# First weight block in four loads, later loads held back, idle products in a gap, a row norm moved to VectorE, four operands re-spaced

## The chip, the cores and the metric

The kernel runs on one core of a Trainium2 chip. The metric is device time in microseconds (us), of which the median of three runs is quoted; one more execution was profiled, and all rows come from that one. Engines: PE (TensorE) does the products, PEld its weight loads, DVE is VectorE, ACT is ScalarE, POOL is GpSimd, SP issues most transfers.

## The reference, cut to what matters

Two transformer blocks run one after the other on 256 rows of width 1024, all in float32. The front of the first block, where most of the change lies, is this:

```python
h = rms_norm(x, norm_mix_g)
proj = h @ w_in
q_d, k_d, v_d, conv_in, q_m, gate_logits = jnp.split(proj, SPLIT_POINTS, axis=-1)
...
mem_n = rms_norm(mem, norm_mem_g)
kv = mem_n @ w_mem_kv
k_m, v_m = jnp.split(kv, 2, axis=-1)
k = rms_norm(k_m.reshape(B, M, MEM_HEADS, MEM_HEAD_DIM), mk_norm_g)
...
y_attn = o.reshape(B, S, DIFF_WIDTH) @ w_attn_o
y_conv = short_gated_conv(conv_in, conv_w) @ w_conv_o
merged = g[:, :, 0] * y_attn + g[:, :, 1] * y_conv + g[:, :, 2] * y_mem
x = x + merged @ w_o
```

After it come an MLP, and a second model with grouped attention, an MLP, a gated block and a last MLP.

## The kernel before

Every float32 matrix is split into a high part and a rest, both in the format fp32r, and a product is three: high by high, high by rest, rest by high. Weights come from memory in units of 1 MB (`raw`, three buffers, loaded by SP). ACT copies each half of a unit to its high part `whi`, DVE subtracts to get the rest `wlo` (lines 86 and 87), seven halves ahead of use at most. The activations are split the same way into pairs of tiles: `memh` (the normed memory), `hT` (the normed input), `cvT`, `oT`, `omT` (convolution, first attention, memory attention), `mgT` (the merged branches), `act` (the MLPs). The two shapes of product are these:

- *Column products* (lines 406 to 408; 488, 489 and 491 in the first one): the activation stands in PE, and 512 columns of weights stream by it.
- *Feature products* (lines 506 to 508): the weights stand, and 256 columns of activation stream by. One group of 24 products shares one half unit.

The order of the work is the program's own order on each engine; `tick()` marks a step after each half unit, and `later(n, f)` puts `f` behind `n` such steps. So PE's work in the first 70 us is: eight idle products of a tile of ones, the transposes of the first 128 rows of the memory (`mt0`), 12 products with the first unit, the transposes of the second 128 rows (`mt1`), the rest of the product with `w_mem_kv` (192 products with `memh` in all), and between them the transposes of small vectors (`vr`), of the keys (`kq`) and of the two halves of the normed input (`kn`). The row norm of the input (`in_norm`, then `norm`) sums squares on ACT and takes the reciprocal root by three Newton steps: on POOL if an engine is handed over, else on DVE in nine instructions. The key norm (`evac_m`, `rsqrt`) takes its root on POOL and is applied by DVE (line 723).

`operands(pool, name, n, skip)` allocates such a pair of tiles with 256 spare bytes, and starts the data `skip` bytes into them. In the built program the split weights all start 64 bytes past a multiple of 128. The distance of each activation from that, modulo 128 bytes, is: `act` and `omT` 0, `hT` 64, `memh` 32, `mgT` 16, `oT` 80, `cvT` 48.

Of the kernel before, what the change touches and what calls it, by code (L numbers as in the profile page):

```python
# [8 lines left out]
F32 = mybir.dt.float32  # L9
# [6 lines left out]
P = 128  # L16
# [7 lines left out]
class Weights:  # L24
# [29 lines left out]
    def load(self, n):  # L54
        while self.loaded < min(n, len(self.plan)):
            t = self.raw_pool.tile([P, 2048], F32, tag="raw", name="raw")
            _, _, src, (a, b) = self.plan[self.loaded]
            v = t.rearrange("p (a b) -> p a b", a=a)
            if self.loaded < 1:
                for h in range(2):  # L60
                    k = slice(h * a // 2, (h + 1) * a // 2)
                    self.nc.sync.dma_start(out=v[:, k], in_=src[:, k])
            else:
                self.nc.sync.dma_start(out=v, in_=src)
            self.raw[self.loaded] = v
            self.loaded += 1
# [4 lines left out]

    def pump(self, n=None):
        while self.split < 2 * len(self.plan) and self.split < min(self.used + self.ahead, n or self.cap):
            self.load(self.split // 2 + self.RAW)
            u, h = divmod(self.split, 2)
            kind, key, _, (a, b) = self.plan[u]
            v = self.raw[u]
            if kind == "B":
                v, shape = v[:, :, h * 128:(h + 1) * 128], (8, 128)
            else:  # L80
                v, shape = v[:, h * a // 2:(h + 1) * a // 2, :], (a // 2, b)
            hi = self.split_pool.tile([P, 1024], F32R, tag="hi", name="whi")
            lo = self.split_pool.tile([P, 1024], F32R, tag="lo", name="wlo")
            hv = hi.rearrange("p (a b) -> p a b", a=shape[0])
            lv = lo.rearrange("p (a b) -> p a b", a=shape[0])
            self.nc.scalar.copy(hv, v)  # L86
            self.rests.append(lambda v=v, hv=hv, lv=lv: self.nc.vector.tensor_sub(lv, v, hv.bitcast(F32)))  # L87
            self.ready.append((kind, key, hv, lv))
            self.split += 1
            if h:  # L90
                del self.raw[u]
# [21 lines left out]
def kernel(  # L113
# [8 lines left out]
    nc = tc.nc  # L122
    V, S, T, G = nc.vector, nc.scalar, nc.tensor, nc.gpsimd
    PSUM = bass.MemoryType.PSUM

    def pool(stack, name, bufs=1, side=None, **kw):
        if side:
            kw["side"] = side
        return stack.enter_context(tc.tile_pool(name=name, bufs=bufs, reuse_waits="tile", **kw))

    const = pool(ctx, "const")

    def operands(p, name, n, skip=0, **kw):

        ts = [p.tile([P, 2048 + 64], F32R, name=f"{name}{i}", **({"tag": f"{name}{i}"} if kw else {}), **kw) for i in range(n)]
        return [t[:, skip // 4:skip // 4 + 2048].rearrange("p (k t) -> p k t", t=256) for t in ts]
# [8 lines left out]
    def bank(p=ps_x):  # L145
        return p.tile([P, 512], F32, tag="bank", name="bank")


    W = Weights(nc, w_raw, w_split)
# [54 lines left out]
    ones = const.tile([P, P], F32, name="ones")  # L204
    V.memset(ones, 1.0)
    xt = [const.tile([P, D], F32, name=f"x{t}") for t in range(NT)]
    hT = [const.tile([P, 8, 256], F32R, name=f"hT{i}") for i in range(2)]
    const.tile([P, 8], F32, name="fill")
    right = ExitStack()
    left = ExitStack()  # L210
    pool(ctx, "edge", side="right").tile([P, 8], F32, name="edge")
# [3 lines left out]
    qmT = memp.tile([P, 8, 256], F32, name="qmT")  # L215
    memin_st = ExitStack()
    memin = pool(memin_st, "memin", side="right")
    memh = operands(memin, "memh", 2, 96)
    mt = [memin.tile([P, D], F32, name=f"mt{t}") for t in range(NT)]
    for n in range(2):  # L220
        nc.sync.dma_start(out=mt[0][:, n * 512:n * 512 + 512], in_=mem[0, 0:P, n * 512:n * 512 + 512])
    W.load(1)
    nc.sync.dma_start(out=mt[1], in_=mem[0, P:2 * P, :])
    W.load(3)

    def rows_of(a):
        return a.rearrange("o (k p) -> (o k) p", p=P)
# [35 lines left out]
    mkg = bc("mkg", mk_norm_g, 256)  # L263
    lam4 = memp.tile([P, 4, 64], F32, name="lam4")
    ssm = memin.tile([P, NT, 2], F32, name="ssm")
    for _ in range(8):
        ps = bank()
        T.matmul(ps[:, 0:P], ones, ones, start=True, stop=True)

    def rsqrt(ss, inv, y, E=None):  # L270

# [23 lines left out]
    def tmp(tag, bufs, n=512):  # L295
        return tmp_pool[0].tile([P, n], F32, tag=tag, name=tag, bufs=bufs)
# [41 lines left out]
    def norm(t, src, ssp, gcol, bcol, dst, E=None):  # L338


        h = small.tile([P, 2], F32, tag="nh", name="nh")
        y = small.tile([P, 1], F32, tag="ny", name="ny")
        if E is not None:
            E.tensor_add(h[:, 0:1], ssp[:, 0:1], ssp[:, 1:2])
            rsqrt(h[:, 0:1], 1.0 / D, y, E)
        else:
            u = small.tile([P, 1], F32, tag="nu", name="nu")
            V.tensor_scalar(h[:, 0:1], ssp[:, 0:1], -0.5 / D, -0.5 * EPS, op0=ALU.mult, op1=ALU.add)
            h = V_stt(h[:, 1:2], ssp[:, 1:2], -0.5 / D, h[:, 0:1], ALU.mult, ALU.add)
            V.tensor_scalar(y.bitcast(I32), h.bitcast(I32), -0.5, RSQRT_SEED - (1 << 22) - (1 << 30), op0=ALU.mult, op1=ALU.add)  # L350
            for _ in range(3):
                V_stt(u, y, h, y, ALU.mult, ALU.mult)
                V_stt(y, u, 1.5, y, ALU.add, ALU.mult)

        def part_2():
            xn = [tmp("kn", 2) for _ in range(2)]
            V.tensor_scalar(xn[0], src[:, 0:512], y, None, op0=ALU.mult)
            S.activation(xn[1], src[:, 512:1024], AF.Identity, scale=y)

            return transposed(t, xn, gcol, bcol, dst)  # L360

        return part_2

    def V_stt(o, a, sc, b, op0, op1):
        V.scalar_tensor_tensor(o, a, sc, b, op0=op0, op1=op1)
        return o
# [6 lines left out]
    def later(n, f):  # L373

        due.append((clock[0] + n, f))
# [23 lines left out]
    def drain():  # L399
        run_due(True)  # L400
        while fillers:
            fillers.popleft()()
        run_due(True)
# [185 lines left out]
    def c1(name, i=0, n=1):  # L589
        v, o = col[name]  # L590
        return vt[v][:, o + i:o + i + n]

    def in_norm(t, src, name, dst):
        ssp = small.tile([P, 2], F32, tag="ssp", name="ssp")
        for n in range(2):
            sumsq(src[:, n * 512:n * 512 + 512], ssp[:, n:n + 1])

        def part_1():
            part_2 = norm(t, src, ssp, c1(name, 0, 8), None, dst, G)
            later(2, lambda: later(3, part_2()))  # L600
        return part_1

    memg = c1("mem", 0, 8)
    mem0, mem1 = (transposed(t, [mt[t][:, n * 512:n * 512 + 512] for n in range(2)], memg, None, memh) for t in range(NT))
# [30 lines left out]
    vecs(0)  # L635

    def mem_mid():
        W.pump(2)
        W.rests.popleft()()
        W.rest()  # L640

    mem0(mem_mid)
    lamneg = const.tile([P, 1], F32, name="lamneg")

    sm = small.tile([P, 2], F32, tag="lsm", name="lsm", bufs=1)
# [23 lines left out]
        later(1, lambda: V.tensor_mul(cond, cond, sig))  # L669

    qkg = const.tile([P, 1], F32, name="qkg")
    later(8, small_setup)
    later(7, lam_sums)
    for i in range(8):
        later(i + 1, lambda: load_smalls(5))
    for t in range(NT):
# [269 lines left out]
    for n in range(2):  # L946
        gemm_cols("in", K0 + 512 * n, hT, evac_k(n))
        gemm_cols("in", Q0 + 512 * n, hT, evac_q(n))
        gemm_cols("in", V0 + 512 * n, hT, evac_v(n))
        if n == 0:  # L950
            drain()
            lam_exp()
            kq_st.close()
            right.close()
            attn_st.close()
            attnp = pool(attn_st, "attnd")
            right = ExitStack()
            oTp = pool(right, "oTp", side="right")
            oT = operands(oTp, "oT", 2, 208)
            kq_p[0] = pool(kq_st, "kq2", side="right")  # L960
            slots(8, [[(0, dif_a)], [(4, dif_ot), (1, dif_b)], [(2, dif_o), (3, dif_n)], [(1, dif_t)]])
    run_due(True)
# [1 line left out]


    convp = pool(right, "conv", side="right")
    cvT = operands(convp, "cvT", 2, 176)
    inner_st = ExitStack()
    inner = pool(inner_st, "inner", side="right").tile([P, 2, 258], F32, name="inner")
    dif_banks[0] = ps_a  # L970
# [1 line left out]
    for f in range(4):  # L972
        xc = tmp("kn", 2).rearrange("p (j c) -> p j c", j=2)
        ps = gemm_feat("in", XC + 256 * f, hT)
        S.copy(xc, ps)
        tick()
        ps = gemm_feat("in", GC + 256 * f, hT)
# [9 lines left out]
        ps = gemm_feat("in", GB + 256 * f, hT)  # L987
# [83 lines left out]
    for f in range(5):  # L1071
        if f < 4:
            branch(G1, 1, "co", cvT, f)
            branch(G2, 2, "mo", omT, f)
        if f == 0:
            cond_silu()
        if f == 1:
            drain()
            attn_st.close()
            qkv_st.close()  # L1080
            ada_p[0] = pool(adap_st, "adap")
            mgp = pool(right, "mgT", side="right")
            mgT = operands(mgp, "mgT", 2, 16)
            for j in range(3):
                ada_load(j)
            ada.extend([lambda: None] * 3)
            for j in range(len(ada_order)):
                ada.append(lambda j=j: ada_step(j))
            clock[1] = 1.04
        if f >= 1:  # L1090
            branch(G0, 0, "ao", oT, f - 1, mgT)
# [345 lines left out]
    for i in range(15):  # L1437
        if i < 12:
            ps = gemm_feat("gin", 256 * i, hT, p=ps_x)
# [72 lines left out]
```

## Time and profile before

| what | value |
|---|---|
| median of three runs | 1320.16 us (1317.58 to 1320.21) |
| the profiled execution | 1320.45 us |
| its span, first to last instruction | 1318.7 us |
| PE busy | 1280.7 us, 97% of the span |
| DVE, ACT, POOL busy | 71%, 55%, 11% |
| mean granted TensorE clock | 0.988 |
| memory traffic | 275.43 MB, mean 209 GB/s |

The span leaves out 1.75 us around it. A share of busy time is a mean over stages. PE's busy time counts a product that is in flight, so two kinds of product at different speeds look equally busy; their speed is read from how many start in a stretch.

### The profile page before, as it was taken

How to read it: one execution, taken by the hardware profiler on the slowest of the kernel's cores; microseconds unless marked ns; L12 is line 12 of the kernel's file. 1: busy time of each engine (PE TensorE's matmuls, PEld its weight loads, DVE VectorE, ACT ScalarE, POOL GpSimd, SP SyncE). 2: the span in 40 equal slices, each digit the busy share in tenths (PEclk: the TensorE clock that was granted, in tenths of full speed). 3: DMA queues.
4: the chain of work that ended last, by engine and by line, in shares of the span. 5: the costliest groups of instructions: out<-in, count | busy, mean ns of one | idle time of the engine just before them, and what ended most of it. 6: DMA issues, size and time to landing. Idle time of an engine off the chain costs nothing.

```text
span 1318.7 us, 20492 instructions
## 1 busy us (share of the span) xinstructions
PE 1280.7 (97%) x7883; PEld 1121.9 (85%) x7883; DVE 929.8 (71%) x1416; ACT 725.7 (55%) x1176; POOL 141.6 (11%) x375
## 2 busy tenths in 40 slices
PE   8899999999999999999878999999999999999998
PEld 6688789999998889977655899987889898799897
DVE  5555678856777788677786787786888877764453
ACT  6765675554444655445555666455556544584451
POOL 1522144500001000100310000000000000000000
PEclk8999999999999999999979999999999999999999
DMA  6573345466885798883431588885886775365650
GB/s 235 201 236 115 129 133 163 158 219 204 276 279 185 225 291 301 275 305 128 158 104 42 190 280 280 294 289 190 282 284 208 264 248 192 119 233 192 223 192 32
DMA packets 166958, 275.43 MB, mean 209 GB/s; under 512 B 8412, under 2 KB 95244, under 8 KB 166732
## 3 DMA queue, kind: packets, MB, share of 16 engines
q1 hardware_dynamic: 137260, 219.78, 49.9%
q10 hardware_dynamic: 27808, 50.41, 11.7%
q0 software_dynamic: 1792, 3.92, 1.1%
q8 instruction: 62, 1.02, 0.3%
q14 instruction: 36, 0.29, 0.1%
HBM read 273.04 MB, written 1.05 MB: 208 GB/s over the span
## 4 chain that ended last, share of the span: by engine, by line
PE 71%; DVE 10%; DMA 8%; ACT 5%; POOL 2%; issue 2%; SPq 0%; ACTq 0%; DVEq 0%; POOLq 0%
PE bank L406 12%; PE bank L407 12%; PE bank L408 12%; PE bank L506 9%; PE bank L507 9%; PE bank L508 9%; DMA araw<-in_ada_w_dram 6%; DVE wlo L87 4%; PE bank L456 2%; ACT whi L86 1%; PE bank L1426 1%; DVE gate L1027 1%; ACT p L1279 1%; PE bank L304 1%; PE bank L447 1%
## 5 line engine op out<-in xcount | busy, mean ns | idle before, releaser
L86 ACT CAST whi<-raw 128x1024 fp32r<-128x1024 f32 x412 | 425.7, 1052 | 267.5 <-PE bank L408 57.9
L87 DVE TENSOR_TENSOR wlo<-raw,whi 128x1024 fp32r<-128x1024 f32 x412 | 496.0, 1220 | 83.5 <-ACT whi L86 82.4
L506 PE MATMUL bank<-hT,whi 128*128 128x256 f32 x1152 | 324.7, 282 | 0.0
L507 PE MATMUL bank<-hT,whi 128*128 128x256 f32 x1152 | 321.2, 279 | 0.0
L508 PE MATMUL bank<-hT,wlo 128*128 128x256 f32 x1152 | 321.2, 279 | 0.0
L506 PEld LDWEIGHTS bank<-hT,whi 128*128 128x128 f32 x1152 | 217.0, 188 | 1.9 <-issue 1.3
L508 PEld LDWEIGHTS bank<-hT,wlo 128*128 128x128 f32 x1152 | 218.2, 189 | 0.0
L507 PEld LDWEIGHTS bank<-hT,whi 128*128 128x128 f32 x1152 | 216.4, 188 | 0.6
L407 PE MATMUL bank<-wlo,act 128*128 128x512 f32 x384 | 150.6, 392 | 2.8 <-DVE wlo L87 2.7
L406 PE MATMUL bank<-whi,act 128*128 128x512 f32 x384 | 150.5, 392 | 0.0
L408 PE MATMUL bank<-whi,act 128*128 128x512 f32 x384 | 150.1, 391 | 0.0
L406 PE MATMUL bank<-whi,hT 128*128 128x512 f32 x308 | 126.9, 412 | 0.8 <-ACT hT L330 0.8
L408 PE MATMUL bank<-whi,hT 128*128 128x512 f32 x308 | 121.6, 395 | 0.0
L407 PE MATMUL bank<-wlo,hT 128*128 128x512 f32 x308 | 121.2, 393 | 0.0
L1027 DVE SCALAR_TENSOR_TENSOR acc<-araw,cond,acc 128x512 f32<-128x512 f32 x128 | 95.7, 748 | 34.6 <-DMA araw<-in_ada_w_dram 34.3
L407 PEld LDWEIGHTS bank<-wlo,act 128*128 128x128 f32 x384 | 72.5, 189 | 19.1 <-DVE wlo L87 4.5
L408 PEld LDWEIGHTS bank<-whi,act 128*128 128x128 f32 x384 | 72.5, 189 | 15.1
L406 PEld LDWEIGHTS bank<-whi,act 128*128 128x128 f32 x384 | 72.4, 188 | 14.6
L406 PEld LDWEIGHTS bank<-whi,hT 128*128 128x128 f32 x308 | 58.2, 189 | 17.5 <-ACT hT L330 4.2
L408 PEld LDWEIGHTS bank<-whi,hT 128*128 128x128 f32 x308 | 58.3, 189 | 13.9 <-DVE hT L319 1.0
L407 PEld LDWEIGHTS bank<-wlo,hT 128*128 128x128 f32 x308 | 58.3, 189 | 12.5 <-issue 1.0
L287 DVE TENSOR_TENSOR act<-s,act 128x512 fp32r<-128x512 f32 x36 | 24.9, 692 | 48.0 <-ACT act L286 47.9
(302 smaller groups left out, 1872.8 us busy)
## 6 DMA issues: line engine op xcount, KB each, us to landing
araw<-in_ada_w_dram ACTq DMA_DIRECT2D x192, 256.0 KB
raw<-in_w_in_dram SPq DMA_DIRECT2D x40, 1024.0 KB
raw<-in_mlp_w_in_dram SPq DMA_DIRECT2D x32, 1024.0 KB
raw<-in_mlp_w_out_dram SPq DMA_DIRECT2D x32, 1024.0 KB
raw<-in_gmlp_w_in_dram SPq DMA_DIRECT2D x24, 1024.0 KB
raw<-in_w_mlp_in_dram SPq DMA_DIRECT2D x16, 1024.0 KB
raw<-in_w_mlp_out_dram SPq DMA_DIRECT2D x16, 1024.0 KB
raw<-in_gmlp_w_out_dram SPq DMA_DIRECT2D x12, 1024.0 KB
```

What stands on the lines that cost most here:

```text
L86: self.nc.scalar.copy(hv, v)
L87: self.rests.append(lambda v=v, hv=hv, lv=lv: self.nc.vector.tensor_sub(lv, v, hv.bitcast(F32)))
L287: V.tensor_sub(lo, src, hi.bitcast(F32))
L304: T.transpose(pss[g][:, j * P:(j + 1) * P], xn[g][:, j * P:(j + 1) * P], ident)
L406: T.matmul(acc, xh, wh, start=start, stop=False)
L407: T.matmul(acc, xh, wl, start=False, stop=False)
L408: T.matmul(acc, xl, wh, start=False, stop=stop)
L456: T.matmul(acc[c][0], act[e][:, k, 0:P], w[0][:, j, :], start=(k + e == 0), stop=False)
L506: T.matmul(acc[:, j], wh[:, k, :], act[0][:, k, :], start=(k == 0), stop=False)
L507: T.matmul(acc[:, j], wh[:, k, :], act[1][:, k, :], start=False, stop=False)
L508: T.matmul(acc[:, j], wl[:, k, :], act[0][:, k, :], start=False, stop=(k == 7))
L1027: V.scalar_tensor_tensor(acc, ada_st.pop(j), cond[:, k:k + 1], acc, op0=ALU.mult, op1=ALU.add)
```

## The change

It has five parts.

1. The first unit of weights comes in four loads of 256 KB (it was two of 512 KB), and the cast of its first half is done in two pieces. The loads of `mt1` and of the next two units, which stood right behind it on SP, are issued from `mem_mid` instead: DVE writes one column of `mt1` there (`memset`), behind the first splits of `memh`, and the load of `mt1` has to wait for that write, with the two units behind it.
2. Four idle products are put between the transposes of `mt0` and the first product.
3. `in_norm` no longer hands over POOL, so the root for both halves of the input is taken on DVE.
4. The transposes of small vectors stand one step later (9 for 8), the sums for `lam` four later (11 for 7).
5. The skips of `memh`, `oT`, `cvT` and `mgT` are now 64, 192, 192 and 0. Distances modulo 128 become 0, 64, 64 and 0. `fill` grows by the 128 bytes that the small tiles of part 3 gave up, so that all other large tiles stay where they were.

```diff
             if self.loaded < 1:
-                for h in range(2):
-                    k = slice(h * a // 2, (h + 1) * a // 2)
+                for k in range(a):
                     self.nc.sync.dma_start(out=v[:, k], in_=src[:, k])
...
-            self.load(self.split // 2 + self.RAW)
+            if self.split > 1:
+                self.load(self.split // 2 + self.RAW)
...
-            self.nc.scalar.copy(hv, v)
+            if self.split == 0:
+                for j in range(2):
+                    self.nc.scalar.copy(hv[:, j], v[:, j])
+            else:
+                self.nc.scalar.copy(hv, v)
...
-    const.tile([P, 8], F32, name="fill")
+    const.tile([P, 40], F32, name="fill")
...
-    memh = operands(memin, "memh", 2, 96)
+    memh = operands(memin, "memh", 2, 64)
...
-    nc.sync.dma_start(out=mt[1], in_=mem[0, P:2 * P, :])
-    W.load(3)
...
-    for _ in range(8):
-        ps = bank()
-        T.matmul(ps[:, 0:P], ones, ones, start=True, stop=True)
+    def keep_busy(n):
+
+        for _ in range(n):
+            ps = bank()
+            T.matmul(ps[:, 0:P], ones, ones, start=True, stop=True)
+
+    keep_busy(8)
...
-            part_2 = norm(t, src, ssp, c1(name, 0, 8), None, dst, G)
+            part_2 = norm(t, src, ssp, c1(name, 0, 8), None, dst)
...
     def mem_mid():
+        V.memset(mt[1][:, 0:1], 0.0)
+        nc.sync.dma_start(out=mt[1], in_=mem[0, P:2 * P, :])
+        W.load(3)
         W.pump(2)
         W.rests.popleft()()
         W.rest()
 
-    mem0(mem_mid)
+    mem0(mem_mid, lambda: keep_busy(4))
...
-    later(8, small_setup)
-    later(7, lam_sums)
+    later(9, small_setup)
+    later(11, lam_sums)
...
-            oT = operands(oTp, "oT", 2, 208)
+            oT = operands(oTp, "oT", 2, 192)
...
-    cvT = operands(convp, "cvT", 2, 176)
+    cvT = operands(convp, "cvT", 2, 192)
...
-            mgT = operands(mgp, "mgT", 2, 16)
+            mgT = operands(mgp, "mgT", 2, 0)
```

On SP, the start of the program before:

```order
L221 DMA mt_98<-in_mem_dram 128x512 x2
L62 DMA raw<-in_w_mem_kv_dram 128x2x512 x2
L223 DMA mt_99<-in_mem_dram 128x1024
L64 DMA raw<-in_w_mem_kv_dram 128x4x512 x5
L242 DMA mqg<-in_mq_norm_g_dram 128x256
```

and now:

```order
L225 DMA mt_98<-in_mem_dram 128x512 x2
L61 DMA raw<-in_w_mem_kv_dram 128x512 x4
L645 DMA mt_99<-in_mem_dram 128x1024
L63 DMA raw<-in_w_mem_kv_dram 128x4x512 x5
L244 DMA mqg<-in_mq_norm_g_dram 128x256
```

The order is the same and the first unit is in four; the third row is the one that now waits for DVE, and everything below it waits with it.

On DVE, between two uses of the key norm (line 723 before, 732 now; `lam` and `lsm` are the sums that move, `vt` the transposed small vectors, `nh`, `nu` and `ny` the small tiles of the input's norm, `x_78` its first half), before:

```order
L723 SCALAR_TENSOR_TENSOR kq<-kq,rsk,mkg 128x256 x4
L87 TENSOR_TENSOR wlo<-raw,whi 128x1024
L654 TENSOR_TENSOR lam_119<-lam_119 128x128
L655 TENSOR_REDUCE lsm<-lam_119 128x2
L87 TENSOR_TENSOR wlo<-raw,whi 128x1024
L584 COPY vt_138<-bank 128x96
L584 COPY vt_139<-bank 128x74
L650 SCALAR_TENSOR_TENSOR qkg<-vt_139 128x1
L87 TENSOR_TENSOR wlo<-raw,whi 128x1024
L357 TENSOR_SCALAR kn<-x_78,ny 128x512
L723 SCALAR_TENSOR_TENSOR kq<-kq,rsk,mkg 128x256 x4
```

and the same place now, as far as the copies of the small vectors:

```order
L91 TENSOR_TENSOR wlo<-raw,whi 128x1024
L354 TENSOR_SCALAR nh<-ssp 128x1
L371 SCALAR_TENSOR_TENSOR nh<-ssp,nh 128x1
L356 TENSOR_SCALAR ny<-nh 128x1
L371 SCALAR_TENSOR_TENSOR nu<-ny,nh 128x1
L371 SCALAR_TENSOR_TENSOR ny<-nu,ny 128x1
L371 SCALAR_TENSOR_TENSOR nu<-ny,nh 128x1
L371 SCALAR_TENSOR_TENSOR ny<-nu,ny 128x1
L371 SCALAR_TENSOR_TENSOR nu<-ny,nh 128x1
L371 SCALAR_TENSOR_TENSOR ny<-nu,ny 128x1
L91 TENSOR_TENSOR wlo<-raw,whi 128x1024 x2
L590 COPY vt_135<-bank 128x96
```

The sums for `lam` are gone from here (they stand behind the second half's norm now), and nine small instructions have come in; a second nine stand behind the next `kq` row. POOL's list loses the fifteen instructions for each half.

## Rows read from the trace of the kernel before

**Rows 1.** Who PE waited for, 0 to 70 us: total, times, longest.
```profile
PE bank L488 <- ACT whi L86: 3.5, 1, 3.5
PE bank L583 <- DMA lam<-in_lam_q_dram: 1.5, 1, 1.5
PE bank L689 <- DVE kq L723: 1.3, 1, 1.3
PE bank L304 <- DVE hf L316: 1.2, 1, 1.2
```

**Rows 2.** Stretches: length, PE busy (instructions), granted clock, DMA share, GB/s.
```profile
4.80:8.20 3.40, 1.22 (x10) 1.00 0.91 286
8.20:15.00 6.80, 5.44 (x13) 0.50 1.04 394
```

**Rows 3.** PE in order of time: start, duration, what, idle time before.
```profile
1.06 3.79 PE L268 MATMUL bank<-ones 128*128 128x128 f32 x16 [1.06 <-DVE ones L205]
...
9.56 0.80 PE L488 MATMUL bank<-whi,memh 128*128 128x512 f32 x1 [3.54 <-ACT whi L86]
...
14.84 1.13 PE L304 MATMUL bank<-ident,mt 128*128 128x128 f32 x8
```

**Rows 4.** DVE's first splits of `memh`; ACT and DVE on the first weights.
```profile
6.70 0.94 DVE L319 TENSOR_TENSOR memh<-hf,memh 128x256 fp32r<-128x256 f32 x2
...
8.46 1.04 ACT L86 CAST whi<-raw 128x1024 fp32r<-128x1024 f32 x1 [1.27 <-DMA raw<-in_w_mem_kv_dram]
9.54 1.23 DVE L87 TENSOR_TENSOR wlo<-raw,whi 128x1024 fp32r<-128x1024 f32 x1 [1.89 <-ACT whi L86]
...
9.80 1.04 ACT L86 CAST whi<-raw 128x1024 fp32r<-128x1024 f32 x1 [0.30 <-DMA raw<-in_w_mem_kv_dram]
```

**Rows 5.** The first half of the input: its issue on SP, its first reader.
```profile
34.28 0.35 SPq L677 DMA_DIRECT2D x<-in_x_dram  x1
...
38.74 0.63 ACT L291 ACTIVATE kn<-x 128x512 f32<-128x512 f32 x1 [1.88 <-DMA x<-in_x_dram]
```

**Rows 6.** POOL, ACT and DVE around the norms, in order of time.
```profile
40.15 1.37 POOL L344 TENSOR_TENSOR nh<-ssp 128x1 f32<-128x1 f32 x1 [1.53 <-ACT kn L291]
...
43.59 0.20 ACT L291 ACTIVATION_READ_ACCUMULATOR kn<-bank,rmem 128x1 f32 x1
...
46.38 1.28 POOL L277 TENSOR_SCALAR rh<-mss 128x4 f32<-128x4 f32 x1
...
52.08 0.74 PE L689 MATMUL bank<-ident,kq 128*128 128x128 f32 x4 [1.32 <-DVE kq L723]
...
58.21 0.49 DVE L357 TENSOR_SCALAR kn<-x,ny 128x512 f32<-128x512 f32 x1 [2.82 <-POOL ny L283]
```

**Rows 7.** A later row norm on DVE, second and last step of it.
```profile
414.38 0.16 DVE L365 SCALAR_TENSOR_TENSOR nh<-ssp,nh 128x1 f32<-128x1 f32 x1 [0.79 <-ACT kn L291]
...
416.11 0.49 DVE L357 TENSOR_SCALAR kn<-x,ny 128x512 f32<-128x512 f32 x1
```

**Rows 8.** Stretches of one kind of product each, columns as in Rows 2.
```profile
25.45:36.65 11.20, 11.20 (x49) 1.00 0.71 250
398.65:418.25 19.60, 19.60 (x87) 1.00 0.62 205
470.38:492.18 21.80, 21.80 (x98) 1.00 0.93 299
...
268.61:274.33 5.72, 5.72 (x51) 1.00 1.03 335
274.33:279.78 5.45, 5.45 (x50) 1.00 0.50 167
279.78:285.52 5.74, 5.74 (x50) 1.00 0.71 236
313.36:319.08 5.72, 5.72 (x51) 1.00 0.88 291
495.00:506.30 11.30, 11.30 (x98) 1.00 0.92 333
```

## The prediction, made before the changed kernel was run

> **What bounds the kernel now.** I began with PE's share: 97% of the span in flight, so whatever shortens PE's own list, or lets it start earlier, reaches the end unless something else is waiting there. Then I asked which waits PE still has where the change lies, before 70 us: four, of 3.5, 1.5, 1.3 and 1.2 us [rows 1]. Then the granted clock: full from 4.8 to 8.2 us, 0.50 of it (1.2 GHz) from 8.2 to 15.0 us, behind a stretch in which PE was busy 1.22 of 3.40 us [rows 2]. Last, since 97% hides speed, I counted products in stretches that hold one kind each. Column products: `memh` 48 in 11.20 us, 233.3 ns each; `mgT` 84 in 19.60, 233.3; `act` 96 in 21.80, 227.1. Feature products: `cvT` 48 in 5.72, 119.2; `hT` 48 in 5.45, 113.5; `omT` 48 in 5.74, 119.6; `oT` 48 in 5.72, 119.2; and `hT` at another place 96 in 11.30, 117.7 [rows 8] (the view counts two or three more, in flight at the edges). The speed goes with the tile, and for `hT` it has two values.
>
> **A, the first products.** Today both halves of the first unit are cast when their load lands, 8.46 and 9.80 us, so 1.34 us per 512 KB or 0.67 per quarter [rows 4]. If the quarters keep that pace, they land at 7.8, 8.5, 9.1 and 9.8. A cast of 512 columns is taken as half of 1.04, so the first product can start at 7.8 + 0.5 + 0.1 = 8.4 instead of 9.56 [rows 3, 4]. Then it waits again: the second half is complete at 9.8 as before, is cast by 10.84, and its rest, 1.23 us on DVE, is ready at 12.1. The last two of the twelve products need that rest and take 0.47 at 233 ns: the block ends at 12.6. Today the transposes behind it start at 14.84 [rows 3], since twelve products at half clock took 5.28 us. So A is 2.2 us, if the clock stays up. If it falls as today, the same list at 0.43 us a product is bound by PE: 10.84 + 8 x 0.43 = 14.3, and A is 0.6. I take 2.2, since the idle products come exactly into the empty stretch: sixteen halves took 3.79 us at the start [rows 3], so eight take 1.9 at most, and end by 7.9, before the weights. They cost nothing there.
>
> The transfers held back: DVE is through with its two first splits at 6.70 + 0.94 = 7.6 us [rows 4] and SP then issues `mt1`. The nearest row is the input, also 512 KB in rows of 4 KB: 4.46 us from issue to its reader [rows 5]. So `mt1` is there at about 12.2, before the 12.6 at which it is wanted; the two 1 MB units follow at some 2.6 us each by the pace above, 14.8 and 17.4. The second is wanted when the twelve products of `mt1` with the first are done, 12.6 + 1.1 for the transposes [rows 3] + 12 at 233 ns, 16.5 at the earliest: still covered. Should the transfer take a third longer, A falls to about 0.9.
>
> **B and C, the small vectors and the key norm.** The transposes of the vectors wait 1.5 us for a load [rows 1]; one step later is 12 products, 2.8 us: gone. The next wait, for the keys at 52.08 us, ends when POOL has taken the root. ACT had the sums at 43.8, POOL began at 46.38, because it was busy with the input's root from 40.15 on, fifteen instructions [rows 6]. Without them it begins with the sums. These hang on the input's load and SP's list, whose head waits for the early splits, so they come earlier by A: 41.6. POOL's root and all behind it move by 46.38 - 41.6 = 4.8 us. PE by itself would be earlier by A 2.2, B 1.5, the 1.3 of this wait, and 145 faster `memh` products (0.9), 5.9 in all: so this chain decides, and at 52 us the gain is **4.8**, B being contained in it. Bounds: 3.2 with A at 0.6, 5.9 if POOL has slack.
>
> **D, the second half's root.** On DVE it costs 8 steps in 1.73 us [rows 7] behind the key norm, so it is ready near 50 instead of the 58.21 at which DVE and ACT go on today [rows 6]. What is queued behind these steps on DVE is the next rests; PE has up to seven halves ahead, and DVE had idle gaps of 2.8 us there [rows 6], so I price the steps at nothing (1.9 each if the cover is gone). PE's 1.2 us [rows 1] mostly goes: **1.0** (0.5 to 1.2), since the buffers of the first half's transposes must also be freed.
>
> **E to G, the distances.** The `memh` products after 52 us, 47 of them, from 233.3 to the 227.1 of `act`, which stands at the same distance 0: **0.3**. `mgT`, 96 at 6.2 ns: **0.6**. `cvT` and `oT` come to `hT`'s distance, 384 products from 119.2 to between 113.5 and 117.7 [rows 8]: 2.2 or 0.6, I take **1.2**.
>
> A rule of the Trainium skill speaks against all three. The page SBUF — State Buffer, section "Who interferes with whom", says that TensorE has two independent read ports, one for the moving operand and one for weight loads, and that PE never waits on anyone; by it a distance between the operands could not matter, and these 2.1 us would be 0. The rows differ by tile at one clock, so I go by them, and keep the rule's outcome as a rival.
>
> **Sum.** 4.8 + 1.0 + 0.3 + 0.6 + 1.2 = 7.9 us. No later stage takes it back: loads are issued when a buffer comes free, so they move along with PE. Against its own 1320.45 us that is 1312.5; that execution is 0.3 above the median of 1320.16, so I forecast **1312.3**. About 0.2% (2.6 us, also the spread of the three runs shown) is what can be told from no change.
>
> **Rivals.**
>
> - *The clock falls anyway.* Nothing in the trace says how much work keeps it up; it fell behind 1.22 of 3.40 us, and the eight halves add 1.9 at most. A is 0.6, the chain gives 3.2: 1313.9.
> - *Distances do nothing,* the speeds follow something else that goes with the tile or its place. Against it: `hT`, `act` and `memh` each hold their speed wherever I looked. 4.8 + 1.0 remain: 1314.4.
> - *`hT` falls to its slow speed between 274 and 396 us.* There its 22 groups of 24 all ran at the fast one (the first two are the 5.45 us row), each pair behind groups of another distance; from now on `cvT` and `oT` have the same distance as `hT`, and only `omT` stands out. If the fast speed is set by the change of distance, 528 products lose 4.2 ns, 2.2 us, and `cvT` and `oT` gain 0.6 only: 1315.2.
> - *The held-back loads come late,* the one that ends on the other side. Place: the transposes of `mt1`. Each us that `mt1` lands after 12.6 costs one, and as SP's list hangs on the splits, it is not won back. Were the old landing put off by the whole 5 us by which the issue moves, PE would be 1 to 3 us behind today at 16 us and the front's gains would go: about 1318. It ends slower by 0.2% when `mt1` lands past 23 us, eleven after the row's estimate. The free DMA queue behind the first unit speaks against it.
>
> **How the numbers follow.** Chances: forecast 0.45; clock 0.18; distances 0.12; slow `hT` 0.18; late loads 0.07, of which about half is slower. The first three are faster by more than 0.2%, the fourth nearly always, unless other stretches of `hT` fall to their slow speed too. So faster 0.88, same 0.08, slower 0.04. The forecast's best bounds (5.9, 1.2, 2.2) give 1309.9, and groups of `hT` elsewhere may change speed for reasons that I cannot see, 0.1 us a group of 24, some 2 us either way: low 1307.5. The rivals reach 1315.2, with the same 2 us on top: high 1317.
>
> **What would show each step.** A: the first product near 8.4, granted clock 1.00 through 15 us, transposes of `mt1` near 12.6. B to D: no wait of PE at the small vectors or the second `kn`; POOL's key root beginning within 0.3 us of ACT's sums; under 1.5 us of wait at the keys. E to G: `memh` and `mgT` stretches at 227 ns, `cvT` and `oT` at 113.5 or 117.7. The prediction is wrong if `mt1` is waited for, if the clock stays at 0.50 beyond 8.2 us, or if 60 to 1318 us takes longer than before.

## The result, and the profile after

The changed kernel took 1312.05 us, the median of nine runs (1310.17 to 1316.32), against 1318.27 for the kernel before in nine runs as well (1317.38 to 1323.32). The ratio is 0.9949, 95% interval 0.9936 to 0.9962: 6.7 us less, between 5.0 and 8.4. The forecast was 1312.3, or 7.9 us less. The profiled execution took 1312.45 us, with a span of 1310.7.

Whom PE waited for from 0 to 70 us, as in [rows 1]:

```profile
PE bank L698 <- DVE kq L732: 1.6, 2, 1.5
PE bank L589 <- DMA ident<-in_ident_dram: 1.4, 1, 1.4
...
PE bank L494 <- ACT whi L90: 0.8, 1, 0.8
...
PE bank L494 <- ACT whi L88: 0.7, 1, 0.7
PE bank L310 <- DVE hf L322: 0.7, 1, 0.7
```

The wait of 3.5 us for the first weights is in two pieces of 0.7 and 0.8, and the one for the vectors is gone. But the keys are waited for 1.5 us at a place where nothing was waited for before, the second `kn` still 0.7, and a wait of 1.4 us for the identity matrix is new, though no part of the change touches that load's own instruction.

The stretches of [rows 2], then stretches of one kind of product, as in [rows 8] (length, PE busy and instructions, granted clock, DMA share, GB/s):

```profile
4.80:8.20 3.40, 2.21 (x17) 1.00 0.74 248
8.20:15.00 6.80, 4.62 (x21) 1.00 0.81 294
20.48:36.86 16.38, 16.38 (x73) 1.00 0.72 249
264.28:269.93 5.65, 5.65 (x50) 1.00 1.05 345
269.93:275.58 5.65, 5.65 (x50) 1.00 0.54 168
275.58:281.34 5.76, 5.76 (x50) 1.00 0.67 222
281.34:286.81 5.47, 5.47 (x50) 1.00 0.29 87
286.81:292.25 5.44, 5.44 (x50) 1.00 0.91 301
308.89:314.33 5.44, 5.44 (x50) 1.00 0.92 301
392.48:411.54 19.06, 19.06 (x87) 1.00 0.64 215
485.43:502.40 16.97, 16.97 (x146) 1.00 0.91 303
```

The granted clock holds through 15 us, and the products are at full speed there. 72 products of `memh` take 16.38 us, 227.5 ns each; 84 of `mgT` 19.06, 226.9. The feature stretches are, in order: `cvT` 48 in 5.65 (117.7), `hT` 5.65 (117.7), `omT` 5.76 (120), `hT` 5.47 (114), `cvT` 5.44 (113.3), `oT` 5.44 (113.3), and `hT` 144 in 16.97 (117.8). So `cvT` and `oT` now run at the two speeds of `hT`.

**Where the time came from.** Since both profiles hold the same products in the same order, I took for five of them how much earlier each starts than in the profile of before, in which they start at 67.65, 268.61, 398.65, 537.32 and 1313.89 us. The table holds all runs told of below.

| run | first `hT` column product | first `cvT` | first `mgT` | an `hT` group | last product |
|---|---|---|---|---|---|
| changed kernel | 4.5 | 4.3 | 6.2 | 6.8 | 8.4 |
| distances alone | 0.7 | 0.6 | 2.5 | 3.0 | 2.6 |
| parts 1 to 4 alone | 5.4 | 5.3 | 5.3 | 5.7 | 6.9 |
| no idle products | 4.8 | 4.8 | 6.6 | 7.6 | 7.3 |
| loads not held back | 5.1 | 5.0 | 6.9 | 7.5 | 9.0 |
| root on POOL | 1.6 | 1.5 | 3.4 | 4.3 | 5.8 |
| `hT` at distance 0 | 5.8 | 5.3 | 4.1 | 3.6 | -2.6 |
| all roots on DVE | 6.3 | 6.3 | 8.1 | 9.1 | 11.4 |
| one product more | 5.8 | 5.8 | 8.1 | 7.4 | 3.3 |
| small sums back | 3.4 | 3.4 | 5.7 | 6.3 | 5.4 |
| two loads | 5.2 | 5.2 | 7.0 | 8.0 | 12.3 |
| roots and input early | 6.8 | 6.6 | 8.5 | 9.1 | 8.1 |

In the changed kernel 4.5 us come from the front, 2.4 from the stretches in which the distances changed, nothing from 430 to 537, and 1.6 behind that. The 1.6 are not the change's: behind 537 us the granted clock falls at other places in every profile. From 590 to 600 us, for instance, it is 0.66 in the run with one product more and 1.00 in the one with two loads:

```profile
590.00:600.00 10.00, 8.64 (x27) 0.66 0.51 167
```

```profile
590.00:600.00 10.00, 10.00 (x50) 1.00 0.56 202
```

The last column moves by up to 4.3 us against the one ahead of it, with the code there unchanged, which is as wide as the scatter of one kernel's times. I therefore read the parts from the columns up to 537 us, and use the times for what is larger. The column at 537 us is itself good to some 0.4 us: a few groups of `hT` ahead of it take either of their two speeds by chance, and parts 1 to 4 alone win 0.4 us there, where nothing was changed.

### The profile page after: what moved, and what is told of

It reads as the page before. It is cut to its first block, busy times and chain, and to the rows that moved or that the text cites. A ratio compares the mean times of both kernels' runs of the same rounds, so it can differ in the third digit from the quotient of the medians.

```text
span 1310.7 us, 20502 instructions
## 1 busy us (share of the span) xinstructions
PE 1274.4 (97%) x7891; PEld 1117.4 (85%) x7891; DVE 931.5 (71%) x1435; ACT 726.1 (55%) x1177; POOL 132.5 (10%) x345
## 4 chain that ended last, share of the span: by engine, by line
PE 72%; DVE 10%; DMA 9%; ACT 5%; POOL 2%; issue 2%; ACTq 0%; SPq 0%; DVEq 0%; POOLq 0%
PE bank L412 12%; PE bank L413 12%; PE bank L414 12%; PE bank L512 9%; PE bank L514 9%; PE bank L513 9%; DMA araw<-in_ada_w_dram 5%; DVE wlo L91 3%; PE bank L462 2%; ACT whi L90 1%; DMA raw<-in_w_mem_kv_dram 1%; DMA raw<-in_attn_w_qkv_dram 1%; ACT p L1288 1%; PE bank L1435 1%; PE bank L453 1%
## 5 line engine op out<-in xcount | busy, mean ns | idle before, releaser
L413 PEld LDWEIGHTS bank<-wlo,hT 128*128 128x128 f32 x308 | 58.0, 188 | 12.9 <-DVE wlo L91 0.8
```

Source lines behind the costliest of these rows:

```text
L413: T.matmul(acc, xh, wl, start=False, stop=False)
```

## The experiments

Each was timed in five rounds beside the kernel before; the ratio is to that kernel.

**The distances alone** (`d1_distances`), the four numbers of part 5 put into the kernel before:

```diff
-    memh = operands(memin, "memh", 2, 96)
+    memh = operands(memin, "memh", 2, 64)
...
-            mgT = operands(mgp, "mgT", 2, 16)
+            mgT = operands(mgp, "mgT", 2, 0)
```

> The kernel before with part 5 alone, the four distances. By my terms E to G: 0.3 + 0.6 + 1.2 = 2.1 us faster than before; by the trace of the changed kernel, where cvT and oT came down to 113.5 ns, nearer 2.8 (1.9 for them, 0.6 for mgT, 0.3 for the last memh), while the faster memh products ahead of 52 us go into the waits that stand there. If the distances do nothing, 0, with memh and mgT at 233 ns and cvT and oT at 119.

Ratio 0.9975 (0.9962 to 0.9989). Between the first `cvT` and 537 us it wins 2.4 us, as the changed kernel does: the distances act without the other parts. Of the 0.7 us in the front, 0.6 stand already at the transposes of `mt1`, because PE was back at full speed by 13.5 us. The faster `memh` products win another 0.6 us by 36 us, and the wait for the vectors, 2.1 us instead of 1.5, takes it back. In this profile the first unit's products from the second to the ninth start 427 ns apart although the granted clock is noted as 1.00 throughout (PE in order of time, then the stretch):

```profile
10.70 0.63 PE L488 MATMUL bank<-whi,memh 128*128 128x512 f32 x1
11.13 0.63 PE L489 MATMUL bank<-whi,memh 128*128 128x512 f32 x1
```

```profile
8.20:15.00 6.80, 5.32 (x20) 1.00 1.04 393
```

So a product's spacing says more of PE's speed in the first 15 us than that column does.

**Parts 1 to 4 alone** (`d2_front`), the changed kernel with the old four numbers:

> The changed kernel with the old distances, so parts 1 to 4 alone. By my terms 4.8 + 1.0 = 5.8 us faster than before; by the trace of the changed kernel, which had won 4.5 us by 70 us, some 4.2. If the 1.6 us that the changed kernel's profiled run won between 550 and 720 us belong to the change and not to that run, they show here or in the run with the distances alone, at the same places of the program.

Ratio 0.9958 (0.9941 to 0.9974). It has won 5.4 us where the products with `hT` begin, as much as the runs with the faster `memh` products and about as early a start (5.1 to 5.8), and nothing from there to 430 us. So in the front the speed of `memh` adds nothing that can be told apart: PE waits 1.3 us for the first keys with the slower products, as it waits 1.5 in the changed kernel.

**Without the idle products** (`d3_no_idle`):

```diff
-    mem0(mem_mid, lambda: keep_busy(4))
+    mem0(mem_mid)
```

> The changed kernel without the four idle products. If they hold the clock up, the granted clock falls to 0.50 soon after 8 us as it did before the change, the twelve products take over 4 us, the transposes of mt1 begin near 14.3 and PE is 1.6 us late there; of this the wait for the keys at 38 us, 1.5 us long, may swallow nearly all, so the end is between 0.1 and 1.6 us later. If the clock stays up without them, nothing changes anywhere.

Ratio 0.9953 (0.9937 to 0.9968), not to be told from the changed kernel's. The clock does fall:

```profile
4.80:8.20 3.40, 1.66 (x11) 1.00 0.80 260
8.20:15.00 6.80, 5.55 (x21) 0.75 0.89 318
```

PE reaches the transposes of `mt1` at 13.12 us, where the runs with idle products, full speed and as early a start come at 11.9 to 12.7. So it is 0.4 to 1.2 us late there, not 1.6, because the clock fell for only 3.4 us; and 0.4 to 1.0 of it is left where the products with `hT` begin (4.8 us won against 5.1 to 5.8 in four runs with the same roots and full speed there; the changed kernel's own profile, with a late identity matrix, has 4.5). The swallowing that I expected is not seen: PE did not wait for the first keys in this run. At the end five rounds do not show a difference. Nor do the idle products secure the speed: with them PE still went down to 427 ns a product once, in the run with the small sums back (0.75 over the same stretch). Up to 15 us it stayed up in the nine other runs that have them and in none of the three without, of which only this one differs in nothing else.

**The loads not held back** (`d4_early`): `mt1` and two units issued right behind the first unit, as before, and no `memset`.

> The changed kernel with the load of mt1 and of two units issued at once behind the first unit, as before. If holding them back is what brings the first quarters early, the first product moves from 8.9 back towards 9.5 us and the second half of the unit from 9.8 to 10.4 or later, and up to 0.7 us are lost at 13 us. If holding them back does nothing, or costs, the first product stays and the transposes of mt1 come no later; at the end 0 or a few tenths faster.

Ratio 0.9945 (0.9929 to 0.996). The first product does not wait longer, but the second half of the unit lands later. PE here, then in `f3_x_early`, in which the loads are held back and the identity matrix came as early:

```profile
8.25 0.50 PE L496 MATMUL bank<-whi,memh 128*128 128x512 f32 x1 [0.91 <-ACT whi L88]
...
10.70 0.50 PE L496 MATMUL bank<-whi,memh 128*128 128x512 f32 x1 [1.08 <-ACT whi L90]
```

```profile
7.81 0.51 PE L494 MATMUL bank<-whi,memh 128*128 128x512 f32 x1 [0.74 <-ACT whi L88]
...
9.92 0.50 PE L494 MATMUL bank<-whi,memh 128*128 128x512 f32 x1 [0.85 <-ACT whi L90]
```

Against that run the block is 0.8 us later. In the other six runs with held-back loads and as early an identity matrix the second half's first product starts at 10.0 to 10.5, so holding back brings it 0.2 to 0.8 us forward, and by 70 us the difference is inside the spread of the runs. It costs nothing either: `mt1` was never waited for.

**Two loads for the first unit** (`f2_two_loads`), its first half still cast in two pieces:

```diff
-                for k in range(a):
+                for h in range(2):
+                    k = slice(h * a // 2, (h + 1) * a // 2)
```

> The changed kernel with the first unit in two loads of 512 KB again, the cast of its first half still in two pieces. By my term A the quarters bring the first product about 0.6 us earlier than a half could (0.67 us per quarter, less the cast), while the second half of the unit, on which the end of the block hangs, lands as before: the first product moves back by 0.5 to 0.7 us, the transposes of mt1 by 0 to 0.2, the end by nothing that can be told. If four transfers side by side are what makes the unit land early, the second half lands later too and all behind it with it.

Ratio 0.9946 (0.9932 to 0.9961). PE starts at 8.85, 0.6 to 1.0 later than the four-load runs whose identity matrix did not hold them up (7.8 to 8.3), and the second half is there about as soon as with four, where its first product starts at 9.9 to 10.9:

```profile
8.85 0.50 PE L495 MATMUL bank<-whi,memh 128*128 128x512 f32 x1 [1.23 <-ACT whi L89]
...
10.57 0.50 PE L495 MATMUL bank<-whi,memh 128*128 128x512 f32 x1 [0.47 <-ACT whi L91]
```

The transposes of `mt1` begin at 12.53, among the others (11.9 to 12.9 at full speed), and the front ends at 5.2. So the quarters bring the first product forward, as the prediction said, and earn nothing that is seen: the block hangs on the second half.

**The root back on POOL** (`e5_pool_root`), part 3 undone in the changed kernel, with `fill` at 8 so that the large tiles stay:

```diff
-            part_2 = norm(t, src, ssp, c1(name, 0, 8), None, dst)
+            part_2 = norm(t, src, ssp, c1(name, 0, 8), None, dst, G)
```

> The changed kernel with the input's root back on POOL. By my terms C and D POOL's key root begins behind fifteen instructions again, some 2.6 us later than now, PE waits over 1 us more for the keys at 48 us and about 1 us more for the second kn, and 2.0 to 2.5 us are lost at the end. If the root's engine is hidden by something else that is late there, under 0.5 us are lost.

Ratio 0.9973 (0.9959 to 0.9988): of the 6.7 us, 3.2 are gone. The front falls to 1.6 us. POOL, then PE, in order of time, and the stretch behind it:

```profile
39.11 3.72 POOL L287 TENSOR_TENSOR ru<-ru,rh 128x1 f32<-128x1 f32 x1
...
45.64 0.49 POOL L283 TENSOR_SCALAR rh<-mss 128x4 f32<-128x4 f32 x1
```

```profile
50.43 1.09 PE L698 MATMUL bank<-ident,kq 128*128 128x128 f32 x4 [2.68 <-DVE kq L732]
```

```profile
49.90:53.30 3.40, 2.87 (x13) 0.50 0.09 28
```

The key root begins at 45.64 instead of 41.93, and PE waits 2.7 us for the keys. Two things made the loss larger than the 2.0 to 2.5 us that I expected. A single POOL instruction takes 3.72 us, beside three `wlo` subtractions of DVE (39.29 to 42.78). And behind PE's wait the granted clock fell to 0.50 for 3.4 us: PE was 1.7 us ahead of the kernel before at the keys, and 0.4 some three us later.

**Part 4 undone** (`f1_small_back`):

```diff
-    later(9, small_setup)
-    later(11, lam_sums)
+    later(8, small_setup)
+    later(7, lam_sums)
```

> The changed kernel with part 4 undone: the transposes of the small vectors and the sums for lam where they stood before. By my term B the wait of 1.5 us for the small loads comes back at 36 us, but it is contained in the key chain: the wait for the keys that stands right behind it now (1.5 us at 38.6) shrinks by as much, and the end moves by under 0.3 us. If DVE, which now has the input's root behind the sums and so behind their load, is held up by it, the second keys and the kn come late and 1 to 2 us are lost.

Ratio 0.9952 (0.9938 to 0.9966), not told apart from the changed kernel; but its front ends at 3.4 us, the lowest of the runs with the root on DVE. The vectors are waited for 1.8 us and the first keys behind them not at all, so that wait takes the place of the other, as expected. DVE does wait, and the granted clock fell a second time (DVE, then the stretch):

```profile
42.99 0.29 DVE L663 TENSOR_TENSOR lam<-lam 128x128 f32<-128x128 f32 x1 [1.49 <-DMA lam<-in_lam_k_dram]
```

```profile
38.10:41.50 3.40, 3.40 (x9) 0.50 0.17 53
```

DVE stands 1.5 us for the load of `lam`, with the input's root and the second keys behind it, and these come at 48.61 instead of 47.74. But PE did not wait for them: it came to them at 50.70. What it lost is its own time. The granted clock stood at 0.50 from 10.8 to 14.2 us and, behind the wait for the vectors, from 38.1 to 41.5, and by my estimate each of these 3.4 us at half speed costs some 1.7 us. That is enough for the 1.2 to 2.4 us by which this front is behind the other runs with the input's root alone on DVE (4.5 to 5.8). So no run shows that part 4 is worth anything, or that the root on DVE needs it.

**`hT` at distance 0** (`e8_hT_at_0`), by 64 bytes ahead of it and 64 fewer in `fill`:

```diff
+    const.tile([P, 16], F32, name="pad")
     hT = [const.tile([P, 8, 256], F32R, name=f"hT{i}") for i in range(2)]
-    const.tile([P, 40], F32, name="fill")
+    const.tile([P, 24], F32, name="fill")
```

> The changed kernel with hT moved by 64 bytes, to distance 0. If the distance sets the speed, all 3456 feature products with hT go from 113.5 or 117.8 to the 119.6 ns of omT, no group shows two speeds any more, its 924 column products go from 229.0 to 227.1, and the end is some 10 us later (3456 x 3.6 ns less 924 x 1.9 ns). If the speed goes with the tile or its place in the program, nothing changes.

Ratio 1.0007 (0.9994 to 1.0021), so 7.6 us slower than the changed kernel by the ratios, and 11.0 by the two profiles, with the clock's part in it. The stretches, `cvT`, `hT`, `omT`, and `hT` in the first MLP:

```profile
263.30:268.76 5.46, 5.46 (x51) 1.00 1.04 344
268.76:274.50 5.74, 5.74 (x51) 1.00 0.55 172
274.50:280.26 5.76, 5.76 (x51) 1.00 0.68 222
488.03:505.30 17.27, 17.27 (x146) 1.00 0.92 317
```

All 144 groups of `hT` stand between 119.2 and 120.1 ns, the speed of `omT`, and no group has another. `cvT` and `oT`, at 64 as in the changed kernel, are at 113.3 to 114.3 in all 16 groups. So the speed goes with the distance, at every place of the program.

**One product more ahead of each run** (`e10_odd_product`). It leaves the result as it is: the added product is overwritten.

```diff
             wh, wl = W.get("B", (key, f0))
+            if p is ps_x and T.n != T.last:
+                T.matmul(acc[:, j], wh[:, 0, :], wh[:, 0:2, :], start=True, stop=True)
```

> The changed kernel with one more product of 256 columns at distance 0 (a piece of whi that moves past whi, its result overwritten by the product behind it) ahead of every run of feature products in the second model that stands behind something else. In the changed kernel every run of hT behind column products there is slow (117.8 ns), and every one behind the products of omT at distance 0 is fast (113.5). If what ran just before sets which, the slow runs turn fast and some 60 groups of 24 win 4.3 ns a product, 6 us, less 0.12 us for each added product, 3 to 4 us net. If the speed hangs on something else, the added products cost 2 to 4 us.

Ratio 0.9962 (0.9945 to 0.9978). That is 1.7 us above the changed kernel, and the intervals overlap. My theory fell: behind the products of `act` the runs are slow with the added product as without. Nor is every run behind column products slow, as I had it: at 976 us, behind products of `hT`, it is fast in all twelve profiles with `hT` at 64. The stretch of [rows 8]'s last kind, 144 products in 17.12 us, where the changed kernel took 16.97:

```profile
484.40:501.52 17.12, 17.12 (x146) 1.00 0.91 308
```

**All three roots on DVE** (`e9_dve_roots`), the memory's and the key's too:

```diff
-        rsqrt(ssm[:, :, 0], 1.0 / D, rmem)
+        rsqrt(ssm[:, :, 0], 1.0 / D, rmem, V)
...
-            rsqrt(ss, 1.0 / 256, rs)
+            rsqrt(ss, 1.0 / 256, rs, V if is_k else None)
```

> The changed kernel with the roots of the memory's norm and of the key norm on DVE too. What is late at 38 and 48 us now is POOL, 6.7 us for the memory's root and 4.7 to 5.8 us for each key root. If that chain is all that is late, the waits of 1.5, 0.4 and 0.7 us at the keys and at the second kn go, and 1.5 to 2.6 us are won. If the loads behind SP's list or DVE's own rests are late next, the wait moves to them and the gain is between 0 and 0.5 us.

Ratio 0.9934 (0.9916 to 0.9953). The front ends at 6.3 us, 0.5 to 1.8 more than the changed kernel and its neighbours; the first wait for the keys is gone, and one of 0.8 is left at the second. On ACT the sums of the second keys stand behind the input's load:

```profile
36.12 0.63 ACT L297 ACTIVATE kn<-x 128x512 f32<-128x512 f32 x1 [4.18 <-DMA x<-in_x_dram]
```

**And the input loaded two steps earlier** (`f3_x_early`):

```diff
-        later(3 + t, lambda t=t: nc.sync.dma_start(out=xt[t], ...
+        later(1 + t, lambda t=t: nc.sync.dma_start(out=xt[t], ...
```

> The run with all three roots on DVE, and the loads of the input issued two steps earlier. There ACT waited 4.2 us for the input at 36 us, and behind it stood the sums of the second keys, for which PE waited 0.8 us at 48 us. If that load is what is late next, these waits go and 0.8 to 1.2 us more are won than by the roots alone. If the small loads that it overtakes are late then, PE waits for them at 35 us instead, and nothing or less is won.

Ratio 0.9935 (0.9922 to 0.9949). 0.5 us more by 70 us, which is inside the spread of runs with one front (5.1 to 5.8), and new small waits, as the second theory had it:

```profile
PE bank L310 <- DVE hf L322: 0.8, 1, 0.8
...
PE bank L589 <- DMA vr<-in_gmlp_ln_b_dram: 0.4, 1, 0.4
PE bank L698 <- ACT kmT L703: 0.3, 1, 0.3
```

Both versions beat the kernel before by more than the changed one does in its median ratio; their intervals overlap with its.

## Why the prediction came out right, and where its terms were off

**A.** Forecast 2.2 us at the transposes of `mt1`; 1.99 measured. It came by another split. PE, then ACT, in order of time:

```profile
5.91 0.19 PE L589 MATMUL bank<-ident,vr 8*128 8x8 f32 x1 [1.41 <-DMA ident<-in_ident_dram]
...
8.86 0.50 PE L494 MATMUL bank<-whi,memh 128*128 128x512 f32 x1 [0.74 <-ACT whi L88]
...
10.87 0.50 PE L494 MATMUL bank<-whi,memh 128*128 128x512 f32 x1 [0.77 <-ACT whi L90]
```

```profile
7.37 0.92 ACT L329 CAST memh<-hf 128x256 fp32r<-128x256 f32 x2 [4.00 <-DVE hf L322]
8.19 1.13 ACT L88 CAST whi<-raw 128x512 fp32r<-128x512 f32 x2
```

The first product came at 8.86 instead of 8.4. It did not hang on the load, as the prediction had it: ACT casts the first weights right behind its cast of `memh`, without a wait, and so they hang on the transposes ahead of that. These waited for the identity matrix, which landed 1.1 us later than before. That is chance: with the distances alone, where nothing of the loads is changed, it landed as late (5.79), and in most runs with the new loads by 4.8. In those PE began at 7.8 to 8.3, near the forecast, but by the same road: ACT began the cast at 7.1 to 7.6, with at most 0.2 us of wait for the load, so the first quarter had landed by then and not at 7.8. That the time fits is luck. The second half came as forecast (cast at 9.77, against 9.80). The stretch ran at full speed, which was the larger part; the rival of the fallen clock (1313.9) did not come true here, and the run without idle products, where it fell for 3.4 us, puts its price at 0.4 to 1.0 us in the front, not 1.6.

**B and C, the key chain.** Forecast 4.8 us at 52 us, measured 3.7. ACT, POOL and DVE, as in [rows 6]:

```profile
41.64 0.20 ACT L297 ACTIVATION_READ_ACCUMULATOR kn<-bank,rmem 128x1 f32 x1
```

```profile
41.93 0.19 POOL L283 TENSOR_SCALAR rh<-mss 128x4 f32<-128x4 f32 x1 [3.87 <-DVE ny L371]
...
42.76 1.22 POOL L287 TENSOR_TENSOR ru<-ru,rh 128x4 f32<-128x4 f32 x1
44.06 1.04 POOL L288 TENSOR_SCALAR ru<-ru 128x4 f32<-128x4 f32 x1
...
47.51 0.20 POOL L289 TENSOR_TENSOR rsk<-ru,rsk 128x4 f32<-128x4 f32 x1
```

```profile
42.70 2.36 DVE L91 TENSOR_TENSOR wlo<-raw,whi 128x1024 fp32r<-128x1024 f32 x2
...
47.74 1.67 DVE L732 SCALAR_TENSOR_TENSOR kq<-kq,rsk,mkg 128x256 f32<-128x256 f32 x4 [1.77 <-POOL rsk L289]
```

POOL begins within 0.1 us of ACT's sums, as predicted. The sums came 1.95 us earlier, not 2.2, and so POOL 4.45. Then the root took 5.78 us (41.93 to 47.71) instead of the 5.04 of before, because two of its instructions took over 1 us where their like take 0.2, and both lie beside DVE's `wlo` of 42.70 to 45.06. "POOL's root and all behind it move by 4.8" held for its start and not for its length: of the 1.1 us missing in the chain, 0.35 are the one and 0.74 the other.

A second step was wrong too. The prediction gave PE by itself 5.9 us at this place, so that the chain alone would decide. PE:

```profile
38.64 0.83 PE L698 MATMUL bank<-ident,kq 128*128 128x128 f32 x4 [1.46 <-DVE kq L732]
...
48.37 0.74 PE L698 MATMUL bank<-ident,kq 128*128 128x128 f32 x4 [0.19 <-DVE kq L732]
```

PE waited only 0.19 us for the second keys, so by itself it was 3.9 us early and not 5.9. It had lost 1.46 at the first keys, which the sum left out. Their chain starts with the memory's root on POOL, which began 1.5 us earlier than before (24.56 against 26.07) and ended 0.6 earlier, since it took 6.7 us instead of 5.8; so DVE's first keys came at 38.10 instead of 38.66, when PE had won 4.1. A faster second root alone would have given PE 0.2 us. With all roots on DVE the first wait is gone, and PE has won 5.5 at the second keys.

The run with POOL's root back lost 3.5 us in the front against the run with the loads not held back, near the 2.6 of C and 1.0 of D. That the sums agree is luck: 2.7 went at the keys, behind the one instruction of 3.72 us, and 1.3 in the fall of the clock behind it, while PE's wait at the second `kn` was 0.2 us only. D by itself is not shown there.

The page SBUF — State Buffer of the Trainium skill has this in its section "SBUF: two separate sides": DVE and GpSimd share a port pair that one of them holds for a whole instruction while the other is blocked. The rows agree: the 1.22, 1.04 and 3.72 us of POOL each end 0.05 or 0.06 us behind one of DVE's subtractions.

**D.** Forecast 1.0 us at the second `kn`, and 0.3 for the last `memh` products; measured 0.8 for both (3.7 us ahead at the keys, 4.5 at the first `hT` product). The root's steps on DVE cost nothing that is seen, as priced: PE waits for no `wlo` before 70 us. A wait of 0.7 us stays.

**E to G.** Forecast 1.2 for `cvT` and `oT` and 0.6 for `mgT`, measured 1.8 and 0.6 in the changed kernel, and the same in the kernel before with the distances alone. The size of the first was off: I took a middle between the two speeds of `hT`, and 14 of the 16 groups got the fast one. The rival by which distances do nothing (1314.4) is refuted by that run and by `hT` at distance 0; the ground given against it, that `hT` holds its speed wherever I looked, did not fit [rows 8], where `hT` has two. The Trainium skill's rule that PE waits for no one (SBUF — State Buffer, "Who interferes with whom") does not describe these rows: at one granted clock the same products take 113.3 or 119.6 ns by the start of one operand.

**The rival of the slow `hT`** was half right. In the changed kernel the speed of a run at distance 64 is carried on from what stands ahead of it: `hT` was slow up to 264 us, `cvT` behind it is slow, `hT` behind that too, and 48 products of `omT` at distance 0 end it (the feature stretches above). In the kernel before `cvT` stood at another distance and ended it. So one pair of `hT` groups lost 0.2 us and the first pair of `cvT` won under 0.1 instead of 0.3; the other pairs stayed fast, and the 2.2 us were not lost. The handing on is seen in the other profiles with both tiles at 64 too: this first pair of `cvT` has the speed of the `hT` products ahead of it in all ten, slow in eight and fast in two. One of the two is the run with the small sums back:

```profile
265.18:270.62 5.44, 5.44 (x50) 1.00 1.03 330
```

**The held-back loads** did not come late, as the forecast had it: no trace shows a wait of PE for `mt1`.

The sum at 537 us is 6.8 in the profile against a forecast of 7.9: 1.1 less at the second keys, 0.5 less in D with the last `memh` products, 0.2 lost on the way to the first `cvT`, and 0.6 more in `cvT` and `oT`. The measured 6.7 (5.0 to 8.4) fits it. That the total came so near is in part luck, since terms were off both ways. Two recorded sums are off by 0.1: the third rival makes 1315.1, and the best bounds 1310.0.

## What to carry to other kernels

Follow the chain, not the wait: of the edits in the front only one, the root taken off POOL, showed in the time when it was undone (3.2 of 6.7 us), while four loads and held-back transfers mended waits behind which the same chains came late anyway. And take every place where PE meets a chain into the sum: here the first keys, where nothing waited before, took 1.5 us. An engine that shares something with a busy one is priced by its slow instructions, not its usual ones. Where an engine is busy all the time, count its instructions per stretch: tiles that do the same work at different speeds point to their addresses, and a few bytes can then be worth 2 us, or 8 to 11 when a tile with as many products as `hT` hangs on them.

## What the runs showed of the hardware

At full granted clock a product of 256 columns takes 119.2 to 120.1 ns when its two operands start at the same place modulo 128 bytes (`omT`, and `hT` when it was moved), 118.8 to 119.4 at 48 or 80 bytes (`cvT` and `oT` before), and 113.3 to 114.3 or 117.8 when they stand 64 bytes apart. For 512 columns it is the other way round: 227 at distance 0, 229 at 64 by the median of `hT`, whose products came to 227 when it was moved to 0, and 233.3 at 16 or 32. The two speeds at 64 are a state. Behind 48 feature products at another distance a run was fast each time (11 pairs of `hT` groups before the change, and 8 pairs of `cvT` and `oT` with `hT` at 0). Behind column products of `act` or `omT`, at distance 0, it was slow each time, and behind those of `hT`, at one place, fast. It can change where transposes interrupt a run, and did not at one added product. What sets it stays open; 76 of the 144 groups of `hT` were slow before, each by 0.1 us.

POOL's small instructions, 0.2 us by themselves, took 1.0 to 3.7 us beside DVE's subtractions: there are 65 such rows before 62 us in the eleven profiles with a root on POOL, and each ends 0.05 or 0.06 us behind one of DVE's TENSOR_TENSOR instructions, nearly always a `wlo`.
